# The embedding projection dealt over three handovers of a decoder layer, with deferred low weights

## The chip, the core and the metric

The kernel runs on one core of a Trainium2 chip. The metric is device time in microseconds. TensorE multiplies matrices, VectorE (DVE) and ScalarE (ACT) work element by element, GpSimd (POOL) takes a few additions, SyncE (SP) issues the transfers. Each engine works through its own list of instructions in order, and they wait for each other by semaphores.

## The reference, cut to what matters

One decoder layer in float32 with d_model 2048, on 256 prompt tokens and 8 sample tokens, 264 columns in all. `token_mixer` is an input projection, a causal convolution group, a state-space (SSD) group in eight groups of heads with a gated norm each, and an output projection.

```
def rmsnorm(x, g):
    xf = x.astype(jnp.float32)
    y = xf * lax.rsqrt(jnp.mean(xf * xf, axis=-1, keepdims=True) + EPS)
    return (y * g.astype(jnp.float32)).astype(x.dtype)

def swiglu(x, wg, wu, wd):
    return (jax.nn.silu(x @ wg) * (x @ wu)) @ wd

    h = h + 0.5 * rmsnorm(swiglu(rmsnorm(h, norm_ffn1_pre), w_ffn1_gate, w_ffn1_up, w_ffn1_down),
                          norm_ffn1_post)
    mix, cb, xb, hs = token_mixer(rmsnorm(h, norm_mix_pre), conv_buf, xbc_buf, h0, w_in, ...)
    h = h + rmsnorm(mix, norm_mix_post)
    h = h + 0.5 * rmsnorm(swiglu(rmsnorm(h, norm_ffn2_pre), w_ffn2_gate, w_ffn2_up, w_ffn2_down),
                          norm_ffn2_post)
    gate = jax.nn.sigmoid(rmsnorm(h, norm_ple_pre) @ w_ple_gate)
    h = h + rmsnorm(gate * (p.astype(h.dtype) @ w_ple_proj), norm_ple_post)
```

The embedding projection is `p @ w_ple_proj`: 256 inputs, 2048 outputs. It depends on nothing that the layer computes, so it may be done anywhere ahead of the last line.

## The kernel before

Everything lies feature by token: a tile is 128 features x 264 tokens, and h is 16 such tiles. A column is one output tile of 128 features; it takes one weight tile of 128x128 for each input tile. A float32 product is three matmuls in a faster format (`mm3`, L275): high part of the weight by high and by low part of the input, then low part of the weight by the high part of the input (L277, L278, L279). So a column over 16 input tiles is 48 matmuls, and a column of the embedding projection, with two input tiles, is 6.

Weights come in units of up to 16 tiles, in the order of a list, `PLAN` (L125). `Weights.load` (L152) takes a unit in halves of eight: a DMA on SP into a raw buffer, ScalarE's cast to the high part `whi` (L172), VectorE's subtract for the low part `wlo` (L175). Of each of the three there are 4 buffers, and `next` (L184) loads two units ahead (`AHEAD`).

The stages: first FFN; input projection with SSD and convolution between its columns; output projection; second FFN; the gate of the embedding; the tail, which adds the last term to h and stores it. FFNs and projections run without a break. Between them stand the handovers. There the sum over features of the squares of a stage's output is needed: `SumSq` adds squares (ScalarE) into a running tile `run`, on VectorE or GpSimd, and `total` (L329) multiplies `run`, and the last square on its own, by a matrix of ones in float32 (L339). ScalarE makes the scale from it by Ln and Exp; VectorE applies it, updates h and makes the next stage's input, high and low part, tile by tile (`residual` L475, `split` L282, `make_u` L581, `update_input` L1091). `gemm_first` (L383) then takes the first columns of the next stage, 7 or 8 at once, input tile by input tile, so that it can begin with the first.

At the first handover the sixteen columns of the embedding projection (two units, "pp") stand between the last column of the FFN and the input projection, each copied to a tile and stored in pairs to a buffer in DRAM, `pproj`. There three totals are made: of y, of h times y and of the scaled y (`ysq`, `hy`, `yy`, filled in `done1`, L539). At the second and third handover TensorE is given matmuls that nobody reads, 4 ahead of the last part of the total and 11 behind it (`HANDOVER = (4, 11)`, L44; `warm`, L375).

In the input stage a group's gate ends with a total of three squares (`gate_begin`, `gate_end`, L936 and L944; the tile `run`, L339), which TensorE takes between matmuls of the input projection. In the tail 16 tiles are dealt to GpSimd (`TAIL_GENERAL`), VectorE (`TAIL_VECTOR`) and TensorE with ScalarE (`TAIL_TENSOR`).

The order on each engine is set by a scheduler that plays the program through ahead of the launch; `high_priority`, `issue_after` and `keep_in_program_order` bind it in places.

## Time and profile before

| | |
|---|---|
| median of 3 runs | 2387.05 us (2385.31 to 2389.02) |
| profiled execution | 2383.33 us, span 2381.6 us |
| granted TensorE clock, mean | 0.999 |
| TensorE busy | 2361.7 us (99%), 19534 matmuls |
| VectorE busy | 1576.5 us (66%), 2382 instructions |
| ScalarE busy | 1186.8 us (50%), 1787 instructions |
| GpSimd busy | 178.0 us (7%), 201 instructions |

A matmul's busy time of 0.28 us overlaps the next one's, so the rate is read from the starts. The share of 99% is an average over stages that differ: it hides where TensorE works on things that nobody reads.

### The profile page before, as it was taken

What the parts mean: (1) busy time and instruction counts of PE and PEld (TensorE: products, weight loads), DVE (VectorE), ACT (ScalarE), POOL (GpSimd) and SP (SyncE); (2) the same over time, 40 slices, a digit from 0 to 9 for tenths busy, and PEclk for the clock granted to TensorE, in tenths of its full rate; (3) what the DMA queues carried; (4) which work ended last, traced back from release to release, by engine and by line L of the source; (5) the groups of instructions that cost most, each with busy time, mean ns of one, the idle gap of its engine ahead of it and who ended that gap; (6) DMA issues with size and microseconds to landing.
All of it is one profiled execution on the core that took longest, in us unless ns stands there. A gap on an engine that the chain in (4) does not pass through costs nothing.

```text
span 2381.6 us, 47454 instructions
## 1 busy us (share of the span) xinstructions
PE 2361.7 (99%) x19534; PEld 2342.3 (98%) x19534; DVE 1576.5 (66%) x2382; ACT 1186.8 (50%) x1787; POOL 178.0 (7%) x201
## 2 busy tenths in 40 slices
PE   9999999999999999999999999999999999999998
PEld 9999999999999998999999999999999999999998
DVE  7554455555557888989898965865545655565586
ACT  6444444433446576656565454644444443344465
POOL 1400000000005000000000011000100000000103
PEclk9999999999999999999999999999999999999999
DMA  7655555555555777666765557567666776666563
GB/s 260 217 184 182 184 184 182 185 184 182 184 173 183 257 229 230 215 222 211 224 214 180 180 168 236 163 232 244 227 211 228 238 241 212 221 234 207 179 206 134
DMA packets 163434, 489.89 MB, mean 206 GB/s; under 512 B 25312, under 2 KB 43024, under 8 KB 163216
## 3 DMA queue, kind: packets, MB, share of 16 engines
q1 hardware_dynamic: 161136, 485.81, 62.7%
q8 instruction: 153, 2.51, 0.4%
q10 hardware_dynamic: 2080, 1.04, 0.2%
q14 instruction: 65, 0.53, 0.1%
HBM read 465.65 MB, written 22.42 MB: 205 GB/s over the span
## 4 chain that ended last, share of the span: by engine, by line
PE 94%; DVE 2%; ACT 2%; issue 1%; DMA 1%; SPq 0%; POOL 0%; ACTq 0%; DVEq 0%; POOLq 0%
PE acc L277 30%; PE acc L278 30%; PE acc L279 30%; PE ps L277 1%; PE ps L278 1%; PE ps L279 1%; DVE wlo L175 1%; ACT whi L172 1%; PE ps L339 1%; PE ps L906 1%; DMA wraw<-in_w 0%; PE ps L891 0%; DVE h L241 0%; DMA d_bc<-rows 0%; DVE ych L851 0%
## 5 line engine op out<-in xcount | busy, mean ns | idle before, releaser
L279 PE MATMUL acc<-act,wlo 128*128 128x264 f32 x6128 | 1733.0, 285 | 1.9 <-DVE wlo L175 1.9
L278 PE MATMUL acc<-act,whi 128*128 128x264 f32 x6128 | 1719.9, 282 | 0.0
L277 PE MATMUL acc<-act,whi 128*128 128x264 f32 x6128 | 1703.7, 282 | 2.5 <-ACT whi L172 2.2
L175 DVE TENSOR_TENSOR wlo<-wraw,whi 128x1024 fp32r<-128x1024 f32 (+2 forms) x814 | 978.1, 1204 | 584.9 <-ACT whi L172 581.3
L172 ACT CAST whi<-wraw 128x1024 fp32r<-128x1024 f32 (+2 forms) x814 | 831.4, 1024 | 974.2 <-PE acc L278 682.8
L277 PEld LDWEIGHTS acc<-act,whi 128*128 128x128 f32 x6128 | 1147.5, 189 | 5.1 <-ACT whi L172 2.9
L279 PEld LDWEIGHTS acc<-act,wlo 128*128 128x128 f32 x6128 | 1144.7, 187 | 5.5 <-DVE wlo L175 3.5
L278 PEld LDWEIGHTS acc<-act,whi 128*128 128x128 f32 x6128 | 1146.8, 187 | 1.9 <-issue 0.9
L241 POOL TENSOR_TENSOR run<-run,tmp 128x264 f32<-128x264 f32 x77 | 72.2, 938 | 889.6 <-ACT tmp L268 889.2
L244 DVE SCALAR_TENSOR_TENSOR y<-v,vec,y 128x245 f32<-128x245 f32 (+23 forms) x240 | 106.2, 465 | 0.6
L241 POOL TENSOR_TENSOR s<-s,eap 128x1024 f32<-128x1024 f32 x24 | 47.0, 1960 | 629.6 <-DMA s<-in_hst 534.4
L244 DVE SCALAR_TENSOR_TENSOR s<-bb,xds,s 128x128 f32<-128x128 f32 x192 | 52.7, 346 | 60.0 <-POOL s L241 60.0
L241 DVE TENSOR_TENSOR tmp<-acc,rr 128x264 f32<-128x264 f32 x99 | 42.5, 430 | 50.2 <-PE acc L279 50.2
L286 ACT CAST act<-tmp 128x264 fp32r<-128x264 f32 x104 | 41.9, 411 | 55.6 <-DVE tmp L241 50.9
L241 DVE TENSOR_TENSOR tmp<-tmp,acc 128x264 f32<-128x264 f32 x84 | 35.9, 428 | 39.9 <-PE acc L279 39.4
L241 DVE TENSOR_TENSOR act<-tmp,act 128x264 fp32r<-128x264 f32 x120 | 52.4, 441 | 0.5 <-ACT act L286 0.5
L278 PE MATMUL ps<-act,whi 128*128 128x264 f32 x192 | 52.3, 283 | 0.0
L279 PE MATMUL ps<-act,wlo 128*128 128x264 f32 x192 | 52.1, 284 | 0.0
L268 ACT ACTIVATE tmp<-tmp 128x264 f32<-128x264 f32 x112 | 47.0, 420 | 6.9 <-DVE tmp L241 6.7
L268 ACT ACTIVATE tmp<-y 128x264 f32<-128x264 f32 x67 | 28.0, 425 | 44.7 <-DVE y L241 43.3
L241 POOL TENSOR_TENSOR run<-run,y 128x264 f32<-128x264 f32 x7 | 7.2, 1029 | 576.7 <-ACT run L321 499.2
L241 DVE TENSOR_TENSOR y<-y,acc 128x264 f32<-128x264 f32 x80 | 34.0, 425 | 23.8 <-PE acc L279 23.8
(170 smaller groups left out, 1038.9 us busy)
## 6 DMA issues: line engine op xcount, KB each, us to landing
wraw<-in_w SPq DMA_DIRECT2D x755, 512.0 KB, 4.7
h<-in_hst SPq DMA_DIRECT2D x24, 512.0 KB, 7.4
s<-in_hst SPq DMA_DIRECT2D x24, 512.0 KB, 6.4
out_nss<-s SPq DMA_DIRECT2D x24, 512.0 KB, 3.6
wraw<-in_w SPq DMA_DIRECT2D x35, 256.0 KB, 3.8
wraw<-in_w SPq DMA_DIRECT2D x23, 384.0 KB
ab<-d_cs SPq DMA_DIRECT2D x14, 384.0 KB, 4.8
cbc<-d_bc SPq DMA_DIRECT2D x8, 512.0 KB, 4.9
```

The lines of the kernel that those rows point to most:

```text
L172: self.hi = nc.scalar.copy(hi[:, c:d], raw[:, c:d]).ins
L175: nc.vector.tensor_tensor(out=lo[:, c:d], in0=raw[:, c:d], in1=hi[:, c:d].bitcast(F32), op=ALU.subtract)
L241: return (eng or nc.vector).tensor_tensor(out=out, in0=in0, in1=in1, op=op)
L244: return nc.vector.scalar_tensor_tensor(out=out, in0=in0, scalar=scalar, in1=in1, op0=op0, op1=op1)
L268: i = nc.scalar.activation(out=out, in_=in_, func=func, bias=bias, scale=scale)
L277: nc.tensor.matmul(acc, hi, x[:, 0, :], start=first, stop=False)
L278: nc.tensor.matmul(acc, hi, x[:, 1, :], start=False, stop=False)
L279: traced[0] = nc.tensor.matmul(acc, lo, x[:, 0, :], start=False, stop=last).ins
L286: nc.scalar.copy(t[:, 0, :], x)
L339: m = nc.tensor.matmul(p, ones, s, start=i == 0, stop=last)
L906: nc.tensor.matmul(pd[64 * q : 64 * q + 64, P * c : P * c + P], xdt[c][:, 2 * j + q, :], ab[c][:, 2 * j + q, :], start=True, stop=True,)
```

## The change

- The projection's columns are dealt: 8 at the first handover, 4 at the second, 4 at the third (`PP`). The fillers go. A generator, `embed`, hands out columns in program order; one column stands ahead of the last part of the total (`between`). `pproj` holds 12 columns; the last four are copied straight to the tiles of the tail. p is loaded and split anew for the second and third handover (`load_p`).
- Ahead of the second and third handover the unit of projection weights has buffers of its own (`own`).
- `defer` holds back the low parts, or those and the second high part, of units loaded near the end of a stage; `flush` issues them behind the last addition and the last square.
- In `done1` the product of h and y and the square of the scaled y are made from y and its gain directly, and y is scaled in place last. Totals are kept in program order.
- For the inputs of the FFNs and of the gate the last square is added on VectorE to `run` (`direct=0`), so that their total is one float32 matmul. It stands ahead of the last columns of the last input tile.
- `update_input` makes the first input tile from a product of two gains (`both`), y, the scale and the old h, and updates h[0] later.
- In the tail, TensorE takes tiles 0, 1, 2, 4, 5, 6, 7; tiles 10 and 11 are done one by one; the last tile is scaled behind the Exp; two of TensorE's sums begin inside the total.

```diff
-        plan.append(("pp", [0, 1], list(range(8 * q, 8 * q + 8))))
+    embed(0, PP[0])
...
+    embed(PP[0], PP[1])
     ffn(2)
+    embed(PP[1], KD)
...
+                own = PLAN[i][0] == "pp" and self.own
...
+                    (own or self.pool).tile(
+                        [P, 8, P], t, tag=tag, bufs=1 if own else 4, name=f"{tag}{i}_{a}"
...
+                    if a and defer == "second":
+                        self.later.append(high)
+                    else:
+                        with nullcontext() if behind is None else tc.issue_after(behind):
+                            high()
...
+                    if defer:
+                        self.later.append(low)
+                        continue
                     with nullcontext() if self.hold is None else tc.issue_after(self.hold):
-                        self.lo = keep(
-                            nc.vector.tensor_tensor(
-                                out=lo[:, c:d], in0=raw[:, c:d], in1=hi[:, c:d].bitcast(F32), op=ALU.subtract
-                            )
-                        ).ins
+                        low()
...
+    def flush(self, behind=None):
+        with self.tc.issue_after(behind) if behind else nullcontext(), self.tc.high_priority(offset=1000):
+            self.later.popleft()()
...
+            self.load(defer=defer)
+        if more:
+            self.load(defer="second")
...
+        def total(self, behind=None, keep=lambda ins: ins, between=None):
             p = ps_tile([P, T])
             with tc.issue_after(behind) if behind is not None else nullcontext():
                 for i, s in enumerate(self.parts):
                     last = i == len(self.parts) - 1
-                    if last and idle[0]:
-                        warm(idle[0], d)
-                    m = nc.tensor.matmul(p, ones, s, start=i == 0, stop=last)
-            if idle[1]:
-                tc.keep_in_program_order(m)
-                warm(idle[1], d)
+                    if last and between:
+                        between()
+                    keep(nc.tensor.matmul(p, ones, s, start=i == 0, stop=last))
             return p
...
+                end = late and n == len(kts) - 1
                 for m in range(nm):
-                    i = mm3(accs[m], w[nm * kk + m], xs[kts[n]], n == 0, n == len(kts) - 1)
+                    if end and m == 3:
+                        late()
+                    keep = tc.keep_in_program_order if end and m else lambda ins: ins
+                    mm3(accs[m], w[nm * kk + m], xs[kts[n]], n == 0, n == len(kts) - 1, keep)
                 n += 1
-                if late and n == len(kts) - 2:
-                    late(i)
...
+                acc = gemm_one(mids, list(range(lo, hi)), **(how.get(m, {}) if end else {}))
...
+                        i = tt(ys[m], ys[m], acc, ALU.add)
+                if end:
+                    if ws.later:
+                        ws.flush(i.ins)
                     done(m, ys[m])
+                    while ws.later:
+                        ws.flush(ysq.squared)
+                    if m == 2:
+                        ysq.add_plain(eq)
...
+    def embed(lo, hi, out, **how):
+        w = ws.next(**how)
+        for m in range(lo, hi):
+            acc = acc_tile()
+            for i in range(2):
+                mm3(acc, w[i * (hi - lo) + m - lo], pacts[i], i == 0, i == 1, tc.keep_in_program_order)
+            out(m, acc)
+            yield m
+    def ysq_total(ysq, cols):
+        return ysq.total(traced[0], tc.keep_in_program_order, lambda: next(cols))
...
+        tt(both[:, i : i + 1], V(post), V(pre), ALU.mult, nc.gpsimd)
+    sq = SumSq(KD, eng=nc.vector, direct=0)
...
-    ysq, hy, yy = (SumSq(KD, f"run{i}", ep, urgent=not i) for i in range(3))
+    ysq, hy, yy = (
+        SumSq(n, f"run{i}", ep, urgent=not i, direct=d) for i, n, d in ((0, KD + 1, 1), (1, KD, 0), (2, KD, 1))
...
             table(LN_EXP)
-        act(y, y, AF.Identity, scale=V("ffn1_post", m))
         t = ep.tile([P, T], F32, tag="hy", bufs=3, name=nm("hy"))
-        tt(t, H(m), y, ALU.mult)
+        stt(t, y, gain, H(m), ALU.mult, ALU.mult)
         hy.add_plain(t)
-        yy.add(y)
+        yy.add(y, gain)
+        act(y, y, AF.Identity, scale=gain)
...
+        pacts[:] = [split(pt[:, k, :]) for k in range(2)]
...
     warm(12)
-    ys, eq = ffn(xs, sq, done1)
+    ys, eq = ffn(xs, sq, done1, ysq, {KD - 2: dict(defer="low"), KD - 1: dict(fill=False)})
     load_p()
-    rs = ffn_scale(ysq, eq)
+    cols = embed(0, PP[0], store_column(ep), fill=False)
+    rs = ffn_scale(ysq, cols)
...
-    pproj = dram.tile([P, KD, T], F32, name="pproj")
-    for q in range(2):
-        w = ws.next(fill=False)
-        for m in range(8):
-            acc = acc_tile()
-            mm3(acc, w[m], pacts[0], True, False)
-            mm3(acc, w[8 + m], pacts[1], False, True)
-            if m % 2 == 0:
-                t = ep.tile([P, 2, T], F32, tag="pp", bufs=4, name=nm("pp"))
-            nc.scalar.copy(t[:, m % 2, :], acc)
-            if m % 2:
-                nc.sync.dma_start(pproj[:, 8 * q + m - 1 : 8 * q + m + 1, :], t)
+    for _ in cols:
+        pass
...
+        accs = gemm_pair(list(range(CM)), more=m == KD - 2)
...
+                added = tt(ys[m + i], ys[m + i], accs[i], ALU.add)
...
+        if m == 8:
+            load_p()
+            ws.own = yp
+    ws.flush(added.ins)
+    while ws.later:
+        ws.flush(ysq.squared)
...
         with tc.high_priority():
-            for k in range(5):
-                if k < 4:
-                    residual(k, ys[k], rs, post, tc.keep_in_program_order)
-                if k:
-                    xs.append(split(H(k - 1), V(pre, k - 1), tc.keep_in_program_order))
+            t, x, u = tmp(), act_tile(), tmp()
+            keep_order(stt(t, ys[0], both[:, stage : stage + 1], rs, ALU.mult, ALU.mult))
+            keep_order(stt(x[:, 0, :], H(0), V(pre), t, ALU.mult, ALU.add))
+            keep_order(stt(u, H(0), V(pre), t, ALU.mult, ALU.add))
+            keep_order(tt(x[:, 1, :], u, x[:, 0, :].bitcast(F32), ALU.subtract))
+            xs.append(x)
+            for k in range(1, 5):
+                residual(k % 4, ys[k % 4], rs, post, keep_order)
+                if k > 1:
+                    xs.append(split(H(k - 1), V(pre, k - 1), keep_order))
...
+    cols = embed(PP[0], PP[1], store_column(yp), fill=False)
     with tc.high_priority():
-        rs = rms_scale(ysq.total(idle=HANDOVER), DM)
-    xs, sq = update_input(rs, "mix_post", "ffn2_pre")
+        rs = rms_scale(ysq_total(ysq, cols), DM)
+    for _ in cols:
+        pass
+    xs, sq = update_input(rs, 0)
...
+    ws.own = ctx.enter_context(tc.tile_pool(name="pw", bufs=1))
...
-    ys, eq = ffn(xs, sq, done2)
+        if m == 8:
+            load_p()
+    ys, eq = ffn(xs, sq, done2, ysq, {KD - 1: dict(more=True)})
     assert not bg
     uctx.close()
-    rs = ffn_scale(ysq, eq, HANDOVER)
-    xs, sq = update_input(rs, "ffn2_post", "ple_pre")
+    gp = ctx.enter_context(tc.tile_pool(name="gp", bufs=1))
+    e4 = [gp.tile([P, 4, T], F32, tag="e4", bufs=4, name=nm("e4")) for _ in range(4)]
+    cols = embed(PP[1], KD, lambda m, acc: nc.scalar.copy(e4[m // 4][:, m % 4, :], acc), fill=False)
+    rs = ffn_scale(ysq, cols)
+    for _ in cols:
+        pass
+    xs, sq = update_input(rs, 1)
...
+        if m % 4 == 0 and m < PP[1]:
             with tc.issue_after(ws.dma.ins):
...
-        act(e, e, AF.Identity, scale=V("ple_post", m))
+        if m < KD - 1:
+            act(e, e, AF.Identity, scale=V("ple_post", m))
...
-    for _ in range(3):
-        begin_sum()
+    def begin_sums():
+        for _ in range(2):
+            begin_sum()
+    total = esq.total(keep=keep_order, between=begin_sums)
+    begin_sums()
...
-                store(i, 1)
                 begin_sum()
+            store(k, n)
...
-TAIL_VECTOR = [(0, 2), (2, 1), (3, 1), (4, 2), (6, 2), (8, 2), (10, 2)]
-TAIL_TENSOR = [0, 1, 2, 4, 5]
+TAIL_VECTOR = [(0, 2), (2, 1), (3, 1), (4, 2), (6, 2), (8, 2), (10, 1), (11, 1)]
+TAIL_TENSOR = [0, 1, 2, 4, 5, 6, 7]
```

The scheduler's order changes with it. VectorE at the end of the first FFN, before: y is the FFN's output, hy its product with h, wlo a low part, ps a total, rr a scale.

```order
L241 TENSOR_TENSOR y_149_3357<-y_149_3357,acc_365_8894 128x264
L175 TENSOR_TENSOR wlo137_8_8903<-wraw137_8_8901,whi137_8_8902 128x1024
L241 TENSOR_TENSOR hy_367_8948<-h_4_88,y_149_3357 128x264
L175 TENSOR_TENSOR wlo138_0_8957<-wraw138_0_8955,whi138_0_8956 128x1024
L241 TENSOR_TENSOR y_151_3420<-y_151_3420,acc_369_8954 128x264
L175 TENSOR_TENSOR wlo138_8_8963<-wraw138_8_8961,whi138_8_8962 128x1024
L241 TENSOR_TENSOR hy_371_9007<-h_4_88,y_151_3420 128x264
L241 TENSOR_TENSOR tmp_378_9026<-ps_380_9028,rr_376_9019 128x264
L244 SCALAR_TENSOR_TENSOR tmp_378_9026<-ps_381_9031,tmp_378_9026 128x264
```

The same place after:

```order
L273 TENSOR_TENSOR y_149_3361<-y_149_3361,acc_365_8899 128x264
L195 TENSOR_TENSOR wlo137_0_8902<-wraw137_0_8900,whi137_0_8901 128x1024
L276 SCALAR_TENSOR_TENSOR hy_367_8951<-y_149_3361,vec_75,h_4_88 128x264
L195 TENSOR_TENSOR wlo137_8_8907<-wraw137_8_8905,whi137_8_8906 128x1024
L273 TENSOR_TENSOR y_151_3424<-y_151_3424,acc_369_8959 128x264
L276 SCALAR_TENSOR_TENSOR hy_371_8999<-y_151_3424,vec_75,h_4_88 128x264
L273 TENSOR_TENSOR tmp_380_9028<-ps_382_9030,rr_376_9013 128x264
L276 SCALAR_TENSOR_TENSOR tmp_380_9028<-ps_383_9033,tmp_380_9028 128x264
```

Each addition has moved ahead of a low part of the same unit (wlo137), and no low part of the next unit stands ahead of the last addition, its product and the first use of the scale.

TensorE at the second handover, before: acc is a column's sum, ps the total, ident and ones the constants of the fillers.

```order
L279 MATMUL acc_18324<-act_17264,wlo_8_18193 128x264
L339 MATMUL ps_18393<-run_17890,ones 128x264
L379 MATMUL ps_18392<-ident,ones 128x128 x4
L339 MATMUL ps_18393<-tmp_18390,ones 128x264
L379 MATMUL ps_18392<-ident,ones 128x128 x11
L277 MATMUL acc_18562<-act_18420,whi_0_18256 128x264
```

The same place after; act_18104 and act_18107 are the two tiles of p:

```order
L311 MATMUL acc_18245<-act_17183,wlo_8_18120 128x264
L370 MATMUL ps_18325<-run_17809,ones 128x264
L309 MATMUL acc_18327<-act_18104,whi_0_18183 128x264
L310 MATMUL acc_18327<-act_18104,whi_0_18183 128x264
L311 MATMUL acc_18327<-act_18104,wlo_0_18184 128x264
L309 MATMUL acc_18327<-act_18107,whi_0_18183 128x264
L310 MATMUL acc_18327<-act_18107,whi_0_18183 128x264
L311 MATMUL acc_18327<-act_18107,wlo_0_18184 128x264
L370 MATMUL ps_18325<-tmp_18320,ones 128x264
L309 MATMUL acc_18340<-act_18104,whi_0_18183 128x264
```

One column stands between the two parts of the total and three behind it, where fillers stood.

VectorE in the input stage, the rows that end with group 3's last addition to its gate sum (`run`), before: h, b and c are inputs of the SSD under their convolution, ych and cbc belong to the samples' states, y_11361 is the convolution group.

```order
L175 TENSOR_TENSOR wlo_0_12176<-wraw_0_12174,whi_0_12175 128x1024
L244 SCALAR_TENSOR_TENSOR y_11361<-v_11355,vec,y_11361 128x238
L241 TENSOR_TENSOR run_11962<-run_11962,tmp_11964 128x264
L244 SCALAR_TENSOR_TENSOR h_12044<-acc_12078,vec,h_12044 128x254
L175 TENSOR_TENSOR wlo_8_12182<-wraw_8_12180,whi_8_12181 128x1024
L244 SCALAR_TENSOR_TENSOR h_12044<-acc_12173,vec,h_12044 128x255
L241 TENSOR_TENSOR h_12044<-h_12044,shist 128x8
L175 TENSOR_TENSOR wlo_0_12321<-wraw_0_12319,whi_0_12320 128x1024
L241 TENSOR_TENSOR h_648_12055<-h_648_12055,cbc_11754 128x1024
L244 SCALAR_TENSOR_TENSOR y_11361<-v_11355,vec,y_11361 128x237
L241 TENSOR_TENSOR run_11962<-run_11962,tmp_11967 128x264
```

After, again up to that addition:

```order
L195 TENSOR_TENSOR wlo_0_11905<-wraw_0_11903,whi_0_11904 128x1024
L276 SCALAR_TENSOR_TENSOR b_11872<-acc_11811,vec,b_11872 128x253
L276 SCALAR_TENSOR_TENSOR y_11280<-v_11274,vec,y_11280 128x234
L273 TENSOR_TENSOR run_11881<-run_11881,tmp_11883 128x264
L195 TENSOR_TENSOR wlo_8_11911<-wraw_8_11909,whi_8_11910 128x1024
L273 TENSOR_TENSOR h_631_11896<-h_631_11896,cbc_11673 128x1024
L276 SCALAR_TENSOR_TENSOR h_11963<-acc_11902,vec,h_11963 128x255
L273 TENSOR_TENSOR h_11963<-h_11963,shist 128x8
L276 SCALAR_TENSOR_TENSOR y_11280<-v_11274,vec,y_11280 128x233
L273 TENSOR_TENSOR prod_12226<-b_11872,c_11593 128x8
L273 TENSOR_TENSOR run_11881<-run_11881,tmp_11886 128x264
```

Convolution steps of y, of which there are more, and fewer low parts stand ahead of the addition now.

## Rows read from the trace of the kernel before

**Rows 1.** Stretches: us, each engine's busy us (instructions), TensorE's granted clock, DMA, GB/s.

```profile
840.00:1290.00 450.00, 442.73 (x3659) 428.82 (x3658) 402.73 (x716) 285.50 (x534) 0.00 (x0) 1.00 0.68 216
1490.00:1515.00 25.00, 24.41 (x200) 23.90 (x199) 17.87 (x35) 14.62 (x28) 3.42 (x4) 1.00 0.36 123
2378.00:2381.50 3.50, 0.00 (x0) 0.00 (x0) 0.07 (x1) 0.00 (x0) 0.00 (x0) 0.61 0.66 250
```

**Rows 2.** Timeline, TensorE, first handover: start, us, instruction, idle before it.

```profile
769.79 0.28 PE L279 MATMUL acc<-act,wlo 128*128 128x264 f32 x1
...
784.82 0.52 PE L277 MATMUL ps<-act,whi 128*128 128x264 f32 x3
```

**Rows 3.** Timeline, VectorE, first handover.

```profile
767.99 1.72 DVE L175 TENSOR_TENSOR wlo<-wraw,whi 128x1024 fp32r<-128x1024 f32 x1 [0.84 <-ACT whi L172]
...
773.75 0.42 DVE L241 TENSOR_TENSOR y<-y,acc 128x264 f32<-128x264 f32 x1
...
778.05 0.43 DVE L241 TENSOR_TENSOR tmp<-ps,rr 128x264 f32<-128x264 f32 x1 [2.15 <-PE ps L339]
...
783.51 0.43 DVE L241 TENSOR_TENSOR act<-tmp,act 128x264 fp32r<-128x264 f32 x1
```

**Rows 4.** Timeline, VectorE, end of the sixteen u tiles: low weights, the last low part.

```profile
824.78 3.52 DVE L175 TENSOR_TENSOR wlo<-wraw,whi 128x1024 fp32r<-128x1024 f32 x3
828.21 0.43 DVE L241 TENSOR_TENSOR act<-tmp,act 128x264 fp32r<-128x264 f32 x1
```

**Rows 5.** Timeline, TensorE, second handover and end of its first columns.

```profile
1500.89 0.29 PE L279 MATMUL acc<-act,wlo 128*128 128x264 f32 x1
...
1501.46 1.05 PE L379 MATMUL ps<-ident,ones 128*128 128x128 f32 x8
1502.91 0.71 PE L339 MATMUL ps<-tmp,ones 128*128 128x264 f32 x2 [0.40 <-ACT tmp L268]
...
1506.27 0.51 PE L277 MATMUL acc<-act,whi 128*128 128x264 f32 x2 [0.19 <-ACT act L268]
...
1548.20 0.39 PE L277 MATMUL ps<-act,whi 128*128 128x264 f32 x1 [0.42 <-DVE rr L421]
```

**Rows 6.** Timeline, VectorE and (first row) ScalarE, second handover.

```profile
1501.13 0.83 ACT L172 CAST whi<-wraw 128x768 fp32r<-128x768 f32 x1 [0.39 <-PE acc L278]
...
1501.92 0.42 DVE L241 TENSOR_TENSOR y<-y,acc 128x264 f32<-128x264 f32 x1
...
1504.71 0.49 DVE L244 SCALAR_TENSOR_TENSOR tmp<-y,vec,rr 128x264 f32<-128x264 f32 x1 [1.50 <-ACT rr L268]
...
1516.19 0.48 DVE L244 SCALAR_TENSOR_TENSOR act<-h,vec,act 128x264 fp32r<-128x264 f32 x1
```

**Rows 7.** Timeline, TensorE, third handover.

```profile
2268.70 0.29 PE L279 MATMUL acc<-act,wlo 128*128 128x264 f32 x1
...
2273.97 0.39 PE L277 MATMUL acc<-act,whi 128*128 128x264 f32 x1
```

**Rows 8.** Timeline, TensorE and VectorE, tail.

```profile
2367.31 0.29 PE L279 MATMUL acc<-act,wlo 128*128 128x264 f32 x1
...
2367.64 0.43 DVE L241 TENSOR_TENSOR tmp<-acc,rr 128x264 f32<-128x264 f32 x1 [4.41 <-PE acc L279]
```

**Rows 9.** Timeline, VectorE and TensorE, gate sums of groups 2 and 3.

```profile
963.86 0.43 DVE L241 TENSOR_TENSOR run<-run,tmp 128x264 f32<-128x264 f32 x1
...
965.41 0.61 PE L339 MATMUL ps<-run,ones 128*128 128x264 f32 x2
...
1019.48 0.42 DVE L241 TENSOR_TENSOR run<-run,tmp 128x264 f32<-128x264 f32 x1
...
1022.16 0.61 PE L339 MATMUL ps<-run,ones 128*128 128x264 f32 x2
```

**Rows 10.** Waits, 840 to 1290 us: total us, times, longest.

```profile
PE ps L339 <- DVE run L241: 2.6, 3, 2.1
...
DVE wlo L175 <- ACT whi L172: 30.7, 26, 3.1
```

More of the change, by code (lines that the diff above doesn't have):

```diff
@@ L90, in _plan, with embed @@
     k16 = list(range(KD))
+    def embed(lo, hi):
+        plan.append(("pp", [0, 1], list(range(lo, hi))))
     def ffn(i):
@@ L150, in __init__, with load @@
         self.hold = None
-    def load(self, between=(), then=(), keep=lambda ins: ins):
+        self.later = deque()
+        self.own = None
+    def load(self, between=(), then=(), keep=lambda ins: ins, defer=None):
         tc, nc, i = self.tc, self.tc.nc, len(self.done)
@@ L313, in add @@
                     with tc.high_priority() if self.urgent and self.i == self.n - 1 else nullcontext():
-                        act(s, x, AF.Square)
+                        self.squared = act(s, x, AF.Square, scale=gain).ins
                 self.add_plain(s)
@@ L327, in add_plain @@
             self.i += 1
-        def total(self, behind=None, idle=(0, 0)):
-            d = ps_tile([P, P]) if idle[0] else None
+        def total(self, behind=None, keep=lambda ins: ins, between=None):
             p = ps_tile([P, T])
@@ L563 @@
     with tc.high_priority():
-        pyy, phy = yy.total(), hy.total()
+        pyy, phy = yy.total(keep=keep_order), hy.total(keep=keep_order)
         keep_order(tt(q2, pyy, rs, ALU.mult))
@@ L1079 @@
     for m in range(0, KD, 2):
-        accs = gemm_pair(list(range(CM)))
+        accs = gemm_pair(list(range(CM)), more=m == KD - 2)
         if m < 8:
@@ L1196 @@
     act(rp, rs, AF.Exp, scale=-0.5)
-    act(rs, rs, AF.Exp, scale=-0.5)
+    last = act(rs, rs, AF.Exp, scale=-0.5).ins
+    e = e4[-1][:, 3, :]
+    with tc.issue_after(last):
+        act(e, e, AF.Identity, scale=V("ple_post", KD - 1))
     def pair(t, k, n):
```

98 lines of the change are left out of this document (51 added, 47 removed).

## Prediction

> **What bounds the kernel now.** I read the stretches of the span first, then the handovers instruction by instruction, then the waits of the input stage. In the input stage TensorE is busy for 442.7 of 450 us with 3659 matmuls, one every 0.12 us [rows 1]. Nearly all of them are matmuls that the change keeps, so only places where TensorE stands, or does work that isn't needed, can give anything. Three are the handovers, where a stage's output has to be summed, scaled and added before the next stage has an input. At the first, the last down-projection matmul issues at 769.79 and the first one of the input projection at 784.82, 15.03 us later [rows 2]; at the second it is 1500.89 to 1506.27, 5.38 us [rows 5]; at the third 2268.70 to 2273.97, 5.27 us [rows 7]. The fourth is the tail. Then there is the input stage itself: VectorE is busy for 402.7 of its 450 us [rows 1], TensorE waits for gate sums from it (2.6 us in three waits), and its low-part subtracts wait 30.7 us for ScalarE's casts [rows 10]. There VectorE is nearly as late as TensorE, and its order matters.
>
> I sum changes against the profiled execution (2383.33, span 2381.6); the median shown is 3.7 above it, and I take the same difference off the median.
>
> **First handover.** VectorE reaches the last addition only at 773.75, 3.96 us after the last matmul [rows 2, 3]: the addition ahead of it and three low-part subtracts, two of them waiting for casts, stand before it. In the changed order the addition ahead goes first, and two subtracts and a product are left. The first subtract runs from 767.99 to 769.7, as its cast comes no earlier [rows 3]; a product of 0.4 and a subtract of 1.17 [rows 4] later, at 771.2, comes the last addition, 1.4 after the last matmul. From an addition to the matmul that closes the total is 0.99 (1501.92 to 1502.91), from there to VectorE's first use of the scale 1.80 (to 1504.71) [rows 5, 6]. So VectorE starts on the scale at 1.4 + 0.99 + 1.80 = 4.2 us. From that use to the low part of the first u tile took 5.46 (778.05 to 783.51) [rows 3], and the instructions are the same after the change: 9.6 against 13.72 now, a gain of 4.1. TensorE has less to do in that time: 8 columns of 6 matmuls, 48 x 0.12 = 5.8, and five fp32 totals of 0.45 (from 0.12 after 1500.89 to 1501.46) [rows 5], 2.25. With waits of about half a microsecond it is through near 8.5, a gain of 6.5, and 0.7 more for the sixteenth column, which now stands behind the first input matmuls: 7.2. Which counts? The last low part of the sixteen u tiles is written from 828.21 to 828.64 [rows 4], while TensorE gets to that tile at 784.82 + 0.72 + 15 x 24 x 0.12 = 828.7: VectorE has 0.1 to spare. It must still write sixteen tiles in the same order, so only its own gain comes through: **-4.2** (bounds -4.2 and -7.2).
>
> **Second handover.** Four useful columns take the place of 15 filler matmuls (from 1501.46 on [rows 5]). No subtract stands ahead of the last addition, so it comes 0.33 after the last matmul, as VectorE does in the tail (2367.31 to 2367.64) [rows 8]: the scale would be there at 0.33 + 0.99 + 1.80 = 3.1 instead of 3.82. But on ScalarE a cast of three quarters, 0.83 [rows 6], and the copy of a column now stand between the last square and Ln, some 0.3 of it uncovered: 3.4. Two dependent instructions of 0.49 [rows 6] and some 0.25 of hops, an estimate, lead to the first matmul near 4.6: -0.8. TensorE's own work there, four columns (2.9) and two totals (0.9) with a short wait between, ends at 4.0, so it isn't the bound. But VectorE's queue grows. Up to the low part of tile 5 it has 26 instructions now, 11.48 us (1504.71 to 1516.19) [rows 6]; after the change six more, two of them low-part subtracts (2.0 for a full one and one of three quarters, by the 1.17 of [rows 4]) and four short ones of about 0.4: 3.5. The first four now wait for each other, some 0.3 more. Tile 5 is written at 3.4 + 11.48 + 3.8 + 0.48 = 19.2; the tile is seven columns wide, and TensorE asks for this low part at 4.6 + 112 x 0.12 = 18.0. A stall of 1.1 is new (bounds 0 and 1.5). One fp32 total less gives 0.45 back, and as the next stage's total is placed ahead of the last four columns of its last tile, column 7 no longer waits 0.6 (0.42 of it named at 1548.20) [rows 5]. Sum: -0.8 + 1.1 - 0.45 - 0.6 = **-0.75**.
>
> **Third handover and the rest.** The same edits: -0.7 + 1.1 - 0.45 = **-0.05**. The first FFN's total has one fp32 matmul less: **-0.45**. In the tail two tiles more are added by TensorE, so VectorE has two additions of 0.43 [rows 8] fewer, while a pair that is split costs it some 0.3; ScalarE's share grows by two copies beside it. I take **-0.5** (bounds 0 and -0.9). The two further loads of p and their casts fall where ScalarE is some 60% busy (14.6 of 25 us) [rows 1] and nobody waits for them: 0, or some tenths if a cast of weights stands behind them. So far: -4.2 - 0.75 - 0.05 - 0.45 - 0.5 = -5.95.
>
> **The input stage, which no edit names.** There the scheduler now places TensorE's small work earlier. Group 2's gate total is row 7824 of TensorE's order and becomes 7731; counted from the first input matmul (rows 6437 and 6392) and without the sixteenth column's six matmuls it stands 42 matmuls, 5.0 us, earlier. Its sum is ready at 963.86 + 0.43 = 964.29 and taken at 965.41, 1.1 to spare [rows 9]. VectorE isn't earlier: up to that sum it has one subtract and one multiply of 128x1024 more and one convolution step less, +1.9 (1.17 [rows 4], as much again, and 0.4). So TensorE would stand 5.0 - 1.1 + 1.9 = 5.8 us. Group 3's total is 143 matmuls earlier, 17.2 us, with 2.3 to spare (1022.16 after 1019.48 + 0.42) [rows 9]; but VectorE's list up to it is now 10.9 shorter (since group 2, six subtracts, three multiplies, two reductions and some short steps fewer, four convolution steps more): 4.0. Group 4: 90 matmuls, 10.8, and a list 5.0 shorter: 5.8 at most. Groups 5 to 7 ask for less by the same count. These don't add up as long as a TensorE that is 5.8 late meets the next sum in time; and being late it no longer meets what it waits for now. Of the 7.3 us that it is idle in the stage [rows 1] the longest gate wait, 2.1 [rows 10], is group 1's; of the rest I take 3 to lie behind group 2, an estimate. The cost is between 2.8 (all of these absorbed) and 5.8 (none): I take **+3.8**, with 0 and +12 as far ends.
>
> Sum: -5.95 + 3.8 = -2.15: profiled 2381.2, median **2384.9**.
>
> **Rivals.** *The input stage costs nothing*, because VectorE, too, gets ahead of the moved totals: -5.95, 2381.1. For it: group 3's list is shorter. Against: group 2's is longer.
>
> *Lateness adds up.* Each late matmul frees a weight buffer later, so ScalarE's cast and the subtract behind it come later too, and VectorE already waits 30.7 us for casts [rows 10]. Then groups 2, 3 and 4 cost 5.8 + 4.0 + 5.8 = 15.6, less 3 absorbed: -5.95 + 12.6 = +6.7, 2393.7, slower. It decides from 10.8 us of lateness on. Against: between gates VectorE has convolution steps that nobody waits for at once.
>
> *The first handover gives nothing*, because something else holds VectorE ahead of the last addition: -2.15 + 4.2 = +2.1, 2389.1.
>
> *The clock.* With the fillers gone TensorE could be granted less. In the rows the granted clock is 1.00 through the second handover, fillers and all, and falls only in the last 3.5 us, to a mean of 0.61, after TensorE has stopped altogether [rows 1]. After the change its idle pieces at a handover come to some 0.6 us, against 0.40 ahead of 1502.91 now [rows 5]. If it fell to 1.2 GHz nonetheless, the 21 matmuls of a first tile would take 0.24 instead of 0.12, 2.5 us at each of two handovers: 2389.9. The Trainium skill (TensorE: Matmul & The Clock Gate, HAM oscillation) says that idle gaps between bursts throttle the clock to half and that the next burst starts slow; by it, taking fillers out can cost. No row here shows matmuls at the lower level, and the columns in the fillers' place keep the gaps short.
>
> **How the numbers follow.** The forecast 0.46, no cost in the input stage 0.30, lateness adding up 0.12, nothing from the first handover 0.08, the clock 0.04. A measurement of this kernel can tell 0.2%, 4.8 us. The second case lies 1.2 beyond that bound, and 0.05 of its 0.30 falls inside; the forecast varies by some 2 us (the stalls at tile 5, the waits absorbed, TensorE's bound at the first handover), and 0.07 of its 0.46 falls outside. The third case is slower, the last two the same. Faster 0.32, same 0.56, slower 0.12. The range goes from the second case without the two stalls (2378.9) to the clock (2389.9), each widened by the 1.9 us by which the runs of before stray from their median: 2377.0 to 2391.8. It leaves out the adding up and a little below.
>
> **What would show it.** Right: from the last matmul of the first FFN to the first input matmul near 9 us, then a stall of 2 to 3 us at the last of its sixteen tiles; at the second and third handover no fillers, some 4.6 us, and a wait for VectorE at tile 5; the gate total of group 2 waiting some 5 us for its sum, the later gates little. Wrong: gates of groups 2 to 4 that all wait long, or none; a granted clock under 1.00 behind a handover; a last addition of the first FFN later than 1.5 us after its matmul.

## The result, and the profile after

The change made the kernel slower by 0.21%, some 5 us by the ratio of runs made side by side and 3 by the medians.

| | before | after |
|---|---|---|
| median (12 runs each, side by side) | 2387.53 us | 2390.64 us (2388.19 to 2398.43) |
| ratio after / before | | 1.0021, 95% interval 1.0012 to 1.0030 |
| profiled execution, span | 2383.33, 2381.6 | 2389.80, 2388.1 |
| TensorE matmuls | 19534 | 19470 |

The two profiled executions differ by 6.5, 3.4 more than the medians: that of before was among the fastest of its kernel, 4.2 us under its median, that of after 0.8 under its own. To see where the time went, I compare the issue of the same matmul in both traces, at the borders of the steps that the prediction summed. Each entry below is worked out from two rows of the timelines: the change in lateness since the border before.

| step | predicted | measured | read at |
|---|---|---|---|
| end of first FFN | -0.45 | -0.75 | 769.79, now 769.04 |
| first handover, to the last of the sixteen input tiles | -4.2 | -5.3 | 829.70, now 823.66 |
| input stage and output projection | +3.8 | **+12.4** | 1500.89, now 1507.23 |
| second handover and 760 matmuls behind it | -0.75 | -0.8 | |
| rest of the second FFN | 0 | +1.3 | 2268.70, now 2275.54 |
| third handover and the gate | -0.05 | -0.5 | 2367.31, now 2373.65 |
| tail | -0.5 | +0.2 | span's end |
| sum | -2.15 | +6.5 | |

So the handovers gave at least what they should, and the stage that no edit names took it all and five microseconds more. One trace of each is not that stage's mean. In a second trace with the same order in this stage (the run without fillers, below) the kernel before loses 2.7 in it against the first, and in two more traces with after's order on TensorE, VectorE and ScalarE (the runs with the old first tile and with the old tail) the stage costs 15.0 and 14.2 where it costs 12.4 here. Over these pairs of traces the cost is 9.7 to 15.0 us, all far above the +3.8. The stretches that answer to [rows 1] (us, each engine's busy us and instructions, TensorE's granted clock, DMA share, GB/s):

```profile
840.00:1290.00 450.00, 434.10 (x3557) 420.32 (x3556) 393.62 (x692) 280.66 (x520) 0.00 (x0) 0.99 0.65 212
1497.00:1522.00 25.00, 24.93 (x202) 24.51 (x201) 18.48 (x36) 14.46 (x29) 3.42 (x4) 1.00 0.51 162
```

In the same 450 us TensorE is busy 8.6 us less and gets through 102 matmuls fewer. VectorE is less busy too, by 9.1.

**First handover**, TensorE's timeline, to be read beside [rows 2]: the last matmul of the FFN, the first one on an input tile, the one that waits for the sixteenth tile.

```profile
769.04 0.29 PE L311 MATMUL acc<-act,wlo 128*128 128x264 f32 x1
...
778.41 0.28 PE L309 MATMUL acc<-act,whi 128*128 128x264 f32 x1
...
823.66 0.39 PE L310 MATMUL acc<-act,whi 128*128 128x264 f32 x1 [0.87 <-DVE act L273]
```

VectorE's, beside [rows 3, 4]:

```profile
770.49 0.42 DVE L273 TENSOR_TENSOR y<-y,acc 128x264 f32<-128x264 f32 x1
...
773.33 0.43 DVE L273 TENSOR_TENSOR tmp<-ps,rr 128x264 f32<-128x264 f32 x1 [1.83 <-ACT rr L300]
...
778.54 0.42 DVE L273 TENSOR_TENSOR act<-tmp,act 128x264 fp32r<-128x264 f32 x1
...
823.18 0.42 DVE L273 TENSOR_TENSOR act<-tmp,act 128x264 fp32r<-128x264 f32 x1
```

Counted from 769.04: last addition +1.45 (forecast 1.4), first use of the scale +4.29 (4.2), low part of the first tile +9.50 (9.6). TensorE's first input matmul comes after 9.37 us instead of 15.03, and the gain beyond VectorE's 4.2 is given back at the sixteenth tile.

**Second handover**, TensorE, beside [rows 5]: last matmul, first one on the new input, the stall at tile 5.

```profile
1507.23 0.29 PE L311 MATMUL acc<-act,wlo 128*128 128x264 f32 x1
...
1511.54 0.63 PE L309 MATMUL acc<-act,whi 128*128 128x264 f32 x3
...
1526.23 0.39 PE L310 MATMUL acc<-act,whi 128*128 128x264 f32 x1 [0.85 <-DVE act L276]
```

4.31 us to the first matmul (forecast 4.6) and one stall, 1.13 from issue to issue (forecast 1.1). The granted clock is 1.00 throughout.

**Input stage.** TensorE's waits from 840 to 1290 us (total us, times, longest), beside [rows 10]:

```profile
PE ps L370 <- DVE run L273: 6.3, 1, 6.3
PE ps L886 <- ACT c L300: 3.1, 1, 3.1
PE acc L311 <- DVE wlo L195: 2.7, 3, 1.2
PE ps L933 <- ACT h L300: 1.8, 1, 1.8
PE ps L754 <- ACT tm L750: 1.6, 1, 1.6
```

The first wait is group 2's gate total, the one that the prediction priced at 5.8. (Gates are counted from 1 here, as in the prediction. The code and the expectations count groups from 0, so this gate is their group 1. What is called group 0 below is the code's first group.) Its place on VectorE (beside [rows 9], where the sum's addition stood at 963.86) and on TensorE:

```profile
963.06 1.22 DVE L273 TENSOR_TENSOR h<-h,cbc 128x1024 f32<-128x1024 f32 x1
964.19 0.42 DVE L273 TENSOR_TENSOR run<-run,tmp 128x264 f32<-128x264 f32 x1
```

```profile
958.15 0.29 PE L311 MATMUL acc<-act,wlo 128*128 128x264 f32 x1
964.76 1.22 PE L370 MATMUL ps<-run,ones 128*128 128x264 f32 x2 [6.33 <-DVE run L273]
...
967.06 0.42 PE L310 MATMUL acc<-act,whi 128*128 128x264 f32 x1
967.28 0.42 PE L311 MATMUL acc<-act,wlo 128*128 128x264 f32 x1
```

VectorE's sum is there 0.3 later than before, but TensorE is ready for it at 958.4, 7 us earlier than in before (965.41). And a second thing follows: behind the wait the matmuls issue 0.22 us apart instead of 0.12. The stretches of TensorE alone (us, busy, granted clock):

```profile
955.00:960.00 5.00, 3.44 (x29) 1.00 0.31 103
960.00:965.00 5.00, 0.24 (x1) 0.87 0.66 196
965.00:967.50 2.50, 2.50 (x10) 0.50 0.74 252
967.50:970.00 2.50, 2.50 (x13) 0.50 0.58 188
970.00:972.50 2.50, 2.50 (x21) 0.90 0.09 26
```

After standing 6.33 us TensorE runs at the lower of its two levels, 1.2 GHz, until 970.4. In before the mean over the stage was 1.00 [rows 1].

The second wait is in no term of the prediction. It lies in group 0, 100 us earlier. ScalarE's timeline there, then TensorE's:

```profile
863.06 1.04 ACT L185 CAST whi<-wraw 128x1024 fp32r<-128x1024 f32 x1 [3.43 <-DMA wraw<-in_w]
864.01 0.42 ACT L300 ACTIVATE c<-c 128x264 f32<-128x264 f32 x1
```

```profile
861.11 0.29 PE L311 MATMUL acc<-act,wlo 128*128 128x264 f32 x1
864.48 0.27 PE L886 MATMUL ps<-ident,c 128*8 128x128 f32 x1 [3.09 <-ACT c L300]
```

TensorE waits for `c`, `c` waits on ScalarE behind a cast, and the cast for its weights, which came late. SP's queue says why. After (start, us that the issues span, transfer, count):

```profile
836.71 4.04 SPq L182 DMA_DIRECT2D wraw<-in_w  x2
848.72 0.33 SPq L896 DMA_DIRECT2D cbc<-d_bc  x1
849.15 0.37 SPq L182 DMA_DIRECT2D wraw<-in_w  x1
849.61 2.24 SPq L767 DMA_DIRECT2D dtp<-d_dt  x2
851.90 4.92 SPq L767 DMA_DIRECT2D eap<-d_dt  x2
856.87 1.21 SPq L182 DMA_DIRECT2D wraw<-in_w  x1
```

Before:

```profile
840.27 7.67 SPq L170 DMA_DIRECT2D wraw<-in_w  x4
852.50 0.33 SPq L837 DMA_DIRECT2D cbc<-d_bc  x1
```

`cbc` is read back from DRAM and can't be issued before `d_bc` is written. In the new order SP reaches it one weight half earlier (without the projection's own weights, 303 halves are issued ahead of it now and 304 before), stands at it from 840.8 to 848.7, and what is behind it stands too: from 840.8 to 856.8 one half of weights is asked for, where before four were between 840.3 and 848. The half issued at 856.87 has its like in before at 856.60, though TensorE was some 6 us ahead of before when it came into this stretch: on SP that lead is gone by then. The Trainium skill (DMA: Bandwidth & Descriptors, Anatomy of one DMA) says that a wait for a semaphore is served by the issuing sequencer and not by the DMA engines; the trace agrees, as SP issues nothing in those 7.9 us.

### The profile page after: what moved, and what is told of

It reads as the page before. It is cut to its first block, busy times and chain, and to the rows that moved or that the text cites. A ratio compares the mean times of both kernels' runs of the same rounds, so it can differ in the third digit from the quotient of the medians.

```text
span 2388.1 us, 47326 instructions
## 1 busy us (share of the span) xinstructions
PE 2359.0 (99%) x19470; PEld 2338.0 (98%) x19470; DVE 1577.7 (66%) x2396; ACT 1189.7 (50%) x1791; POOL 186.4 (8%) x206
## 4 chain that ended last, share of the span: by engine, by line
PE 88%; DVE 6%; DMA 4%; issue 1%; ACT 1%; SPq 0%; POOL 0%; ACTq 0%; DVEq 0%; POOLq 0%
PE acc L310 28%; PE acc L309 28%; PE acc L311 28%; DVE wlo L195 2%; DMA wraw<-in_w 1%; DMA d_bc<-rows 1%; DVE h L273 1%; PE ps L311 1%; PE ps L310 1%; PE ps L309 1%; DMA s<-in_hst 1%; ACT whi L185 1%; PE ps L965 0%; DMA cbc<-d_bc 0%; PE ps L950 0%
## 5 line engine op out<-in xcount | busy, mean ns | idle before, releaser
L276 DVE SCALAR_TENSOR_TENSOR y<-v,vec,y 128x251 f32<-128x251 f32 (+23 forms) x240 | 106.9, 468 | 0.9
L310 PE MATMUL ps<-act,whi 128*128 128x264 f32 x192 | 51.9, 281 | 0.0
L309 PE MATMUL ps<-act,whi 128*128 128x264 f32 x192 | 46.2, 283 | 0.0
```

Source lines behind the costliest of these rows:

```text
L276: return nc.vector.scalar_tensor_tensor(out=out, in0=in0, scalar=scalar, in1=in1, op0=op0, op1=op1)
L309: keep(nc.tensor.matmul(acc, hi, x[:, 0, :], start=first, stop=False))
L310: keep(nc.tensor.matmul(acc, hi, x[:, 1, :], start=False, stop=False))
```

## The experiments

Lateness against before at the same matmul, counted from the first input matmul, in the profiled executions (us):

| | k = 500 | 800 | 1200 | 1400 | 1800 | end of output projection |
|---|---|---|---|---|---|---|
| after | -5.9 | -0.45 | -1.2 | +7.65 | +8.75 | +6.35 |
| later gate total | -5.6 | -0.2 | -1.0 | +1.8 | +1.6 | -1.5 |
| weights first | -5.8 | -2.4 | -3.1 | +4.35 | +5.2 | +4.2 |
| both | -5.25 | -3.0 | -2.2 | +1.05 | +0.8 | -1.7 |
| fillers at the gate | -6.0 | +0.5 | 0.0 | +6.7 | +6.5 | +7.55 |

Group 0 lies between the first two columns (+5.4 in after), group 2's gate between 1200 and 1400 (+8.8). The two other traces with after's order in this stage lose 6.1 and 5.9 in the first stretch and 7.8 and 9.7 in the second, so a difference of 1 us between two single traces says little.

**Group 2's gate total one column later** (the wait is taken away by putting 97 matmuls ahead of it).

```diff
-            if g and j == (g == 1):
+            if g and g not in (2,) and j == (g == 1):
+                gate_end(*gated.pop())
+            if g == 2 and j == 1:
                 gate_end(*gated.pop())
```

> The changed kernel, but the gate of group 1 (the second gate total on TensorE) is written one column triple later in the program (with the second x column of the next group and not the first), so that the scheduler places its total behind 1393 input matmuls and not behind 1296 (before: 1338). Theory A, the order of the input stage is the cause: TensorE no longer waits 6.3 us at 964.8, its clock does not fall there (2.3 us more), and since 2.4 us of this came back later in the changed kernel, the time falls by about 6 us, to near 2384.5. Rival B, the stage's end is set by VectorE's and the casts' work whatever TensorE's order is: the wait only moves to a later gate or column, and the time stays within 2 us of the changed kernel's 2390.6.

2383.62 us (2379.59 to 2385.05, 11 runs), ratio to before 0.9983 (0.9974 to 0.9992). The wait for `run` is gone from the list of TensorE's waits (840 to 1290 us), and 7 us of the median with it:

```profile
PE ps L886 <- ACT c L300: 4.1, 1, 4.1
PE acc L311 <- DVE wlo L195: 3.7, 4, 2.0
...
```

One total, asked for too early, is what turned a gain into a loss. The wait for `c` stays. Not all of the gate's price is gone: between matmuls 1200 and 1400 this run still loses 2.8 (8.8 in after), and there TensorE waits 1.22 and 2.02 for low parts.

**Weights ahead of `cbc`** (the load of `cbc` is written where the loads of `dtp` and `eap` were, and these a column earlier, so that SP comes to the weights first).

```diff
             if g == 1:
+                load_dt()
                 state_times_c(0, 0)
...
                 do_tokens(dt, dta, cs)
-                load_cbc(0)
...
             if g == 1:
                 ws.hold = None
-                load_dt()
+                load_cbc(0)
```

> The changed kernel, but on SP's queue the load of group 0's broadcast c (cbc) stands behind one more half unit of weights, and the loads of the sample tokens' dt behind one unit more, as it was before the change or a little later. Theory A: the weights' cast at 863.06 no longer waits 3.4 us for its transfer, c's SiLU behind it on ScalarE comes 3 us earlier, TensorE's wait of 3.1 us at 864.5 and the half clock behind it (1.6 us) go: 3 to 5 us less up to there. Gate 2 stays as it is, and as VectorE is what it waits for, between nothing and all of this is left at the end: 2386.5 to 2390.5. Rival B: no change at the end of the stage, 2390.6 within 1 us, and TensorE waits longer at gate 2 by what it gained.

2389.85 us (2386.31 to 2395.16, 11 runs), 1.0013 (1.0004 to 1.0022). On SP one weight half more now goes ahead of `cbc`, as many as in the kernel before, and ScalarE's cast and `c` come 6.4 us earlier than in after (863.06 and 864.01 there):

```profile
856.67 1.04 ACT L185 CAST whi<-wraw 128x1024 fp32r<-128x1024 f32 x1
857.66 0.43 ACT L300 ACTIVATE c<-c 128x264 f32<-128x264 f32 x1
```

TensorE doesn't wait for `c` any more. In group 0 that is worth 2.0 us (-2.4 instead of -0.45 at matmul 800), not all 5.4: behind 870 us it now waits for VectorE, 0.5 and 1.2, and the granted clock there is 0.85 and 0.81 over stretches of 5 us. The gate still waits 6.2: TensorE comes to it 2 us earlier (956.2), but so does VectorE's last addition (962.10), and the longer wait of rival B does not come. The two ratios, 1.0021 and 1.0013, say the same 2 us, but their intervals overlap, so by the times alone the edit isn't shown to help.

**Both.**

> Both edits of the last two runs together. Theory A: the input stage loses only what little the tokens' sums (1.8 us at 844) and the later gates take: about 10 us less than the changed kernel, near 2381, faster than the kernel before by some 6 us. Rival B: within 3 us of the changed kernel, 2388 to 2392.

2381.19 us (2377.58 to 2386.4, 10 runs), 0.9975 (0.9964 to 0.9985). Against the changed kernel that is 9 us by the medians and 11 by the ratios. What is left, -5.9 against before by both, is near the sum of the prediction's terms outside the input stage (-5.95): with the stage repaired the handovers' gain shows in the time. That the two figures agree so well is luck in part: in its own trace the stage still loses 4.0 against the trace of before, and 2.2 in a second trace of the same kernel (the last run below).

**Fillers at the gate.** 32 matmuls that nobody reads stand ahead of group 2's total, so that TensorE is busy where it stood.

```diff
-        rsqrt(t, sq.total(traced[0]), eps1, 1.0 / 384)
+        fill = None
+        if g == 1:
+            d = ps_tile([P, P])
+
+            def fill():
+                for _ in range(32):
+                    keep_order(nc.tensor.matmul(d, ones, sq.last[:, :P], start=True, stop=True))
+
+        rsqrt(t, sq.total(traced[0], keep_order if fill else (lambda ins: ins), fill), eps1, 1.0 / 384)
```

> The changed kernel with 32 float32 filler matmuls of 128 columns (4.2 us, read by nobody) ahead of the second gate's total, so that TensorE stands 2 us there and not 6.3. Theory A with the clock as a part of it: the total still issues when its sum is ready, near 965, but the granted clock stays at 1.00 behind it and the 20 or so matmuls up to 970 issue every 0.12 us and not every 0.22: 2.3 us less, 2388. Without a part of the clock: the same time as the changed kernel. Some small works of the next groups stand up to 50 matmuls later by this edit, so the stretch behind the gate is the thing to read, not the total alone.

2389.63 us, one run. The fillers, each of them two instructions on TensorE, took 7.06 us (957.48 to 964.54) and not 4.2 as expected, so they cover the whole wait:

```profile
957.48 7.31 PE L1013 MATMUL ps<-tmp,ones 128*128 128x128 f32 x64
```

The same stretches as above:

```profile
960.00:965.00 5.00, 5.00 (x47) 1.00 0.74 235
965.00:967.50 2.50, 2.50 (x22) 1.00 0.69 223
967.50:970.00 2.50, 2.50 (x23) 1.00 0.12 34
```

Clock 1.00, and 22 and 23 matmuls in 2.5 us instead of 10 and 13: 22 more in 5 us, which at 0.12 each are 2.6 us. Between matmuls 1200 and 1400 the kernel loses 6.7, 0.3 less than the fillers took; after loses 8.8, 2.5 more than its wait of 6.33. So some 2.6 of the gate's price is the clock, the rest the wait. The total of this run says nothing, since group 0 happened to cost 1.0 more.

**The first input tile as before.** `update_input` of the kernel before, the rest as changed.

```diff
-            t, x, u = tmp(), act_tile(), tmp()
-            keep_order(stt(t, ys[0], both[:, stage : stage + 1], rs, ALU.mult, ALU.mult))
...
+            for k in range(5):
+                if k < 4:
+                    residual(k, ys[k], rs, post, tc.keep_in_program_order)
+                if k:
+                    xs.append(split(H(k - 1), V(pre, k - 1), tc.keep_in_program_order))
```

> The changed kernel with the input of the second and third handover made as in the kernel before (h[0] updated first, no product of the gains); the input stage is untouched, so only the two handovers are read. In the changed kernel the first matmul issues 4.30 and 4.20 us after the stage's last, and TensorE then stands 1.13 at tile 5 both times. Theory A (the early first tile is given back at tile 5): the first matmul comes some 0.4 later (near 4.7) and the stall falls to 0 to 0.4, so both handovers are together 0.3 to 1.2 us shorter. Theory B (the stall comes from the held-back low parts alone): the stall stays near 0.7 to 1.1, and the handovers are the same or up to 0.8 longer.

2394.78 us, one run; only the handovers are read. The first matmul comes 5.08 and 5.11 us after the last one (4.31 and 4.20 in after), later by twice what was expected, and the stall at tile 5 is gone, as theory A has it. Up to the 760th matmul the third handover is 0.4 shorter (96.86 from the last matmul, 97.27 in after), as in theory A. The second is 2.7 longer (100.65, 97.94): there the next FFN's total now waits 1.9 for its sum (0.3 in after), and behind that wait the clock is 0.66 over 5 us. Most of the 2.7 is that clock: with both repairs, the old first tile and the old tail (below) the same wait of 1.90 is met at a clock of 1.00, and the second handover takes 99.10, against 98.35 with both repairs alone. The third takes 96.88 there, so its 0.4 comes again. So the early first tile gives 0.8 to 0.9, tile 5 takes it back, and at the second handover it saves the later wait, which neither theory had.

**Before, without fillers.**

```diff
-HANDOVER = (4, 11)
+HANDOVER = (0, 0)
```

> The kernel before without the 15 filler matmuls at the second and third handover, and nothing in their place. Theory A (the clock holds through a handover of some 4 us): the first matmul stays 5.0 to 5.4 us after the stage's last, the first tile's matmuls follow 0.12 apart, the time is within 1 us. Theory B (the clock falls as it does behind the 6.3 us at group 2's gate): the windows behind the two handovers show a granted clock near 0.5, matmuls 0.22 apart for some 4 us, and the stage comes about 2 us later at each.

2388.49 us, one run. The first matmul stays at 5.38 and 5.28 us, but theory B is right about the clock. TensorE's timeline and the stretches behind the second handover:

```profile
1505.94 0.71 PE L339 MATMUL ps<-tmp,ones 128*128 128x264 f32 x2 [1.29 <-ACT tmp L268]
1509.30 0.87 PE L277 MATMUL acc<-act,whi 128*128 128x264 f32 x5 [2.65 <-ACT act L268]
...
1510.32 0.42 PE L278 MATMUL acc<-act,whi 128*128 128x264 f32 x1
1510.54 0.42 PE L279 MATMUL acc<-act,wlo 128*128 128x264 f32 x1
```

```profile
1507.50:1510.00 2.50, 0.70 (x5) 1.00 0.64 215
1510.00:1512.50 2.50, 2.50 (x14) 0.53 0.03 7
1512.50:1515.00 2.50, 2.50 (x19) 0.79 0.00 0
```

0.22 us a matmul, and the first 21 are done 1.4 us later than with fillers (9.27 after the last matmul, 7.89 before); at the third handover 1.5. The fillers of the kernel before were worth that; in the changed kernel the columns of the projection do the same service.

**The tail as before**, the rest as changed.

```diff
-TAIL_VECTOR = [(0, 2), (2, 1), (3, 1), (4, 2), (6, 2), (8, 2), (10, 1), (11, 1)]
-TAIL_TENSOR = [0, 1, 2, 4, 5, 6, 7]
+TAIL_VECTOR = [(0, 2), (2, 1), (3, 1), (4, 2), (6, 2), (8, 2), (10, 2)]
+TAIL_TENSOR = [0, 1, 2, 4, 5]
```

> The changed kernel with the tail of the kernel before (5 tiles by TensorE with ScalarE, tiles 10 and 11 as a pair, the last tile scaled ahead of the total). From the last matmul of the gate projection to the end of the span the kernel before takes 14.29 us, the changed one 14.45. As the prediction had it (two additions fewer on VectorE are worth 0.5): this kernel's tail is 0.3 to 0.9 longer than the changed kernel's, 14.8 to 15.3. Rival (the copies by ScalarE and the new waits take back what VectorE is spared): 14.2 to 14.5.

2391.12 us, one run; its tail is 14.4 us, as in after: the new tail gives nothing. In the traces of this study the old one took 14.3 to 14.4 in five. The new one took 14.4 to 14.6 in five and 16.1 in two. In all seven TensorE stands 1.29 for VectorE; in the two the clock fell behind it (the run with both repairs):

```profile
2365.00:2370.00 5.00, 3.33 (x14) 1.00 0.00 0
2370.00:2372.50 2.50, 2.50 (x8) 0.53 0.16 54
2372.50:2375.00 2.50, 2.50 (x11) 0.78 0.71 270
```

**Both repairs, old first tile and old tail.**

> Later gate total and weights ahead of c as in the run that did both (2381.2 median), and in addition the first tile and the tail as in the kernel before. If the early first tile and the new tail give nothing: 2379.5 to 2381.2, that is 0.2 to 0.3% under the kernel before. If each is worth what the prediction gave it (0.35 at each handover and 0.5 in the tail): 2382.0 to 2382.8.

2380.66 us (2377.03 to 2384.44, 10 runs), 0.9973 (0.9963 to 0.9982): as the one without the last two edits. Runs that spread over 7 us can't tell this from the 1 us that the other case would add.

**Both repairs and the old tail, beside both repairs alone.**

> Later gate total and weights ahead of c, the changed kernel's first tile, and the tail of the kernel before. In the traces so far the changed tail took 14.45 to 14.57 us four times and 16.1 twice (granted clock 0.53 to 0.55 from 5 to 7.5 us behind the last column), the old one 14.29 to 14.41 every time. Theory A (the new tail sometimes meets a lower clock and gives nothing otherwise): tail 14.3 to 14.5, the median 0.3 to 1.0 us under the run that is the same but for the tail, sent beside it: near 2380.5. Rival (the tail is neutral on the whole): the two within 0.3.

2378.1 us (2376.14 to 2384.58, 7 runs), 0.9975 (0.9961 to 0.9988).

> The kernel with the later gate total and weights ahead of c once more, beside the one with the old tail, on the same chip. Median 2380.5 to 2381.9 if the first figure (2381.2) holds; its tail 14.45 or 16.1 us long in the trace.

2380.59 us (2377.65 to 2382.51, 8 runs), 0.9977 (0.9967 to 0.9986); its tail is 14.46 us. The one with the old tail is 2.5 lower by the medians, more than expected, and 0.5 by the ratios. The intervals overlap, so the old tail isn't shown to be better, but nothing speaks for the new one. Each version with both repairs is some 0.25% faster than the kernel before. These two traces also show one reason why executions of one program differ. Up to 875 us both wait for the same things, to 0.2 us. Then the one with the old tail keeps a clock of 1.00, and the other (below) falls to 0.66 and loses 1.6 us more between matmuls 700 and 800:

```profile
870.00:875.00 5.00, 3.35 (x22) 1.00 0.14 52
875.00:880.00 5.00, 5.00 (x29) 0.66 0.80 243
```

## Why the prediction was wrong

It named no change as likeliest (2384.9), and the kernel came out slower, if only just beyond the 0.2%. The time lies within the range, near its upper end.

- **First FFN and handovers: right.** Together -7.4 (forecast -5.45). The first handover was under-sized by 1.1: I had TensorE of before at its sixteenth tile at 828.7, with VectorE 0.1 ahead. That is where the tile's first matmul issues, 360 matmuls on. The first one that needs the low part comes eight later, behind the eight columns' products of the two high parts, and issued at 829.70: VectorE was 1.0 ahead, and this slack was given up too. And TensorE's first input matmul came after 9.37 us, not 8.5, so the stall is 1.15, not 2 to 3. The step that only VectorE's gain counts was right: its last low part came 5.03 earlier (828.21, 823.18), 4.3 of it from the handover. The rival that nothing comes of the first handover is ruled out by this.
- **The failing step is the +3.8 for the input stage.** It measured +12.4 in the traces above (9.7 to 15.0 over the pairs). Its first part was right: group 2's gate waits 6.3 (forecast 5.8), groups 3 to 7 little (the list above has one wait for `run`). By the prediction's own terms TensorE would have been there at 955.8 and the sum at 961.5. Both came some 3 us later, behind group 0's loss, so the near hit is the difference of two times that were both missed. Three things were not right. The wait was priced as its length, while it costs some 2.6 more at the lower clock. I took off 2 us of the 5.8 for other waits that a late TensorE would no longer meet; of the 9.9 us lost between matmuls 1200 and 1800 only 2.4 came back by the end of the output projection. And group 0 was left out: I went through the moved gate totals and not through the queues ahead of them. The row that would have told is in SP's order: `cbc` ahead of a weight half that was ahead of it before. Group 0 cost 5.4 by matmul 800, of which the second experiment takes 2.0 away by order on SP; the rest (the wait for `tm` behind ScalarE's own work, the clock of 0.69 from 865 to 870 us, a wait for VectorE that shows when the first is gone) I have not separated.
- **Lateness adds up (2393.7, +12.6 in this stage): the size of the traces by chance, and the wrong mechanism.** Groups 3 and 4 did not wait. VectorE's waits for casts did grow in this stage, from 30.7 to 37.6 us; with both repairs they are 22.6 to 26.8, so they went with the two stalls.
- **The input stage costs nothing (2381.1)** is the time that the run with both repairs had, 2381.19, partly by luck as said there; the changed kernel's own stage was far from it.
- **The clock: the right mechanism, looked for in the wrong place.** I tested it at the handovers, where the columns keep TensorE busy, and gave it 0.04; it struck behind the long wait in the middle of the input stage. The Trainium skill (TensorE: Matmul & The Clock Gate, HAM oscillation) says that idle gaps throttle the clock to half and that the next burst starts slow. The runs agree: 0.50 behind 6.33 us of standing, and 0.53 in before without fillers, behind 1.29 and 2.65 us with a short total between them.
- **Tail: -0.5 forecast, +0.2 measured.** VectorE has two additions fewer, but TensorE waits 1.29 for VectorE's product (0.40 at that place before), and the stores end no sooner. What bounds the tail I have not settled.
- **Rest of the second FFN: +1.3** in two or three waits for inputs, which no term named. In the other traces it is 0 to 1.1, with the same edits and without, so it lies in the spread of the executions; what makes it differ stays open.

## What to carry to other kernels

When an edit makes a scheduler move work that it doesn't name, follow every queue through the moved stretch, the one that issues transfers first: a transfer that has to wait for a write to DRAM holds all weights behind it (7.9 us here). A wait on TensorE is to be priced at its length plus the slow matmuls behind it. And a total that TensorE shares with its main work should be asked for late: 97 matmuls of distance saved 7 us of the median here.

## What the runs showed of the hardware

- In a kernel whose TensorE is 99% busy the granted clock fell to 0.50 behind a single wait of 6.33 us; matmuls of 264 columns then issued 0.22 us apart for 3.7 us, and the price was some 2.6 us beside the wait. It fell in each of the four traces that have this wait (6.2 to 7.1 us).
- It fell behind shorter stands too, but not each time: with the same waits of 0.5 and 1.15 us ahead of it, one execution kept 1.00 and another fell to 0.66; behind a wait of 1.90 one kept 1.00 and another fell to 0.66; and the clock fell behind the tail's 1.29 us in two traces of seven.
- With matmuls that nobody reads in the gap the clock stayed at 1.00, at the handovers of before as at the gate, in one trace each.
